# Ranking the experts behind the first gather, and letting the first pair of experts take turns from its first chunk

## The chip, the cores and the metric

The kernel runs on one core of a Trainium2 chip. The metric is the time of one execution on the device, in microseconds (us), median of several runs. Matrix products run on TensorE (PE in the profile, its weight loads PEld), elementwise work on VectorE (DVE) and ScalarE (ACT), a little on GpSimd (POOL). SyncE (SP) issues the loads of the weights; ScalarE also issues some stores.

## The reference

Two decoder layers over 256 tokens of width 1024. Layer 0 is gated linear attention and a dense SwiGLU, layer 1 is softmax attention with a forget gate ("fox") and a mixture of 8 experts, two of which serve each token. Each sub-layer has a norm ahead of it with a shift and a scale, and a gate on its residual. The change lies in the experts:

```python
def swiglu(h, w_gate, w_up, w_down):
    return (jax.nn.silu(h @ w_gate) * (h @ w_up)) @ w_down

def moe_swiglu(h, w_router, b_router, w_gate, w_up, w_down):
    logits = (h @ w_router).astype(jnp.float32) + b_router.astype(jnp.float32)
    top_vals, top_idx = lax.top_k(logits, TOP_K)
    top_w = jax.nn.softmax(top_vals, axis=-1)
    combine = jnp.sum(jax.nn.one_hot(top_idx, N_EXPERTS, dtype=jnp.float32)
                      * top_w[..., None], axis=-2)
    y = jnp.zeros_like(h)
    for e in range(N_EXPERTS):
        y = y + combine[..., e:e + 1].astype(h.dtype) * swiglu(h, w_gate[e], w_up[e], w_down[e])
    return y
```

Every expert has a gate and an up matrix of 1024 x 3584 and a down matrix of 3584 x 1024, all float32: 42 MB an expert, 336 MB for all 8 (1 MB = 2^20 bytes).

## The kernel before

The kernel does not compute all tokens with every expert. For each expert it gathers the tokens that chose it into up to 128 slots (large) or up to 64 slots (small), runs the SwiGLU on these, and scatters the result back with the weights of the router. The experts are put into 8 places: place 0 is always expert 0, taken as a large one; the other places are filled by rank, so that places 0, 2, 4, 6 are large and 1, 3, 5, 7 small. Which expert stands in a place is known on the chip only, in the tile `order`; the loads of the weights of place 1 and of all later ones take the expert's number from there, by a load into a register of SP at line 1264 (in `Slot.__init__`).

`route` (line 974) makes the router's logits (`lg`), the mask of the two largest (`msk`), each token's slot within its expert (`pos`), the rows of the tokens as a high and a low part (`hh`, `hl`), and, in `weights` (lines 1035 to 1078), the softmax weights (`comb`), the count of tokens per expert (`cnt`, by two small matmuls at line 1048), the rank of each expert, `order`, the slots and weights in the order of the places (`pos_s`, `comb_s`), and the room of each place (`room`, `cmi`), from which the kernel decides at its end whether a slow path is needed.

`experts` (line 1093) does the rest. `onehot` (line 1111) and `gather` (line 1123) put the tokens of a place into the operand `g` (large) or `gs` (small). The gather of place 0 uses `pos` and needs no rank; that of place 1 uses `pos_s`.

Weights come in units of 1 MB, one load each (`unit`, line 203), into a ring of 10 buffers (7 in one pool, 3 in another that opens with the experts), taken in the order in which the units stand in the program. The feed-forward width is cut into 4 chunks, three of 1024 columns and one of 512. For a large place `gu(c)` (line 1272) is the gate and up products of a chunk: 4 gate units and 4 up units (2 and 2 for the last chunk); `down(c)` (line 1300) is 4 units (2 for the last). Each unit is split into a high part on ScalarE (`whi`, line 224) and a low part, mostly on VectorE (`wlo`, line 226); the split ends the use of its buffer. There are 3 such pairs of parts. A unit is then 12 matmuls of 512 columns (lines 241 to 243). For a small place TensorE reads the unit as it is, in 8 matmuls (line 1249), and these end the use of the buffer. `finish` (line 1229) transposes a chunk's result for the down product; it is put off by `pend` and `flush` to the first unit of the next gate product. The first four splits have an order of their own (`hows`, line 1254), so that they fit around the router and the first gather.

The order of instructions on each engine is set by a planner, which goes through them by priority (the order of the program, with functions marked `urgent` moved up by 400) and by the times that it expects. `after(x)` lets an instruction follow `x` on `x`'s own engine.

In the first pair, places 0 and 1, the order of the program is: gate and up of chunk 0 and of chunk 1 for place 0, then `weights`, the down product of chunk 0, the gather of place 1, and only then place 1's chunk 0; from there the places take turns, place 0 one chunk ahead. The later pairs take turns from their first chunk on.

Of the kernel before, what the change touches and what calls it, by code (L numbers as in the profile page):

```python
# [8 lines left out]
F32 = mybir.dt.float32  # L9
# [15 lines left out]
NCH = 4  # L25
E = 8
# [24 lines left out]
def trunk(ctx, tc, x, c, ada_w, ada_b, norm_gain, gla_w_in, gla_w_gate_up, gla_b_gate, gla_o_norm, gla_w_out,  # L51
          fox_w_in, fox_b_f, fox_q_norm, fox_k_norm, fox_w_out, ffn_w_gate, ffn_w_up, ffn_w_down,
          moe_w_router, moe_b_router, moe_w_gate, moe_w_up, moe_w_down, out):
    nc = tc.nc
# [13 lines left out]
    def urgent(f):  # L68

        def g(*a, **k):  # L70
            with tc.high_priority(URGENT):
                return f(*a, **k)
        return g

    @contextmanager
    def after(*instructions):

        with ExitStack() as es:
            for i in instructions:
                es.enter_context(tc.issue_after(i.ins))  # L80
            yield
# [37 lines left out]
    bias = adap.tile([P, 96], F32, name="bias")  # L119
# [854 lines left out]
    def route(norm, wr):  # L974
        mp = wk
        first = {}
        msk, comb, pos = (cst.tile([P, NB, E], F32, name=n) for n in ("msk", "comb", "rpos"))
        cmi = cst.tile([P, 1], I32, name="cmi")
        order = cst.tile([P, E], I32, name="order")
        comb_s, pos_s = (cst.tile([P, NB, E], F32, name=n) for n in ("comb_s", "pos_s"))  # L980
        room = cst.tile([P, E], F32, name="room")
        hh, hl = (t.rearrange("p k t -> p (k t)")[:, 0:NB * D].rearrange("p (b d) -> p b d", b=NB)
                  for t in pair("Y", "m"))
        lg = mp.tile([P, NB, E], F32, tag="rlg", name="rlg", bufs=1)
# [47 lines left out]
                    nc.vector.scalar_tensor_tensor(hl[:, b, c], ps[2 * b + q], r[:, b:b + 1],  # L1032
                                                   hh[:, b, c].bitcast(F32), op0=ALU.mult, op1=ALU.subtract)

        def weights():
            mx = mp.tile([P, NB], F32, tag="rmx", name="rmx", bufs=1)
            sm = mp.tile([P, NB], F32, tag="rsm", name="rsm", bufs=1)
            nc.vector.tensor_reduce(mx, lg, axis=AX.X, op=ALU.max, negate=True)
            for b in range(NB):
                nc.scalar.activation(comb[:, b, :], lg[:, b, :], AF.Exp, bias=mx[:, b:b + 1])  # L1040
            nc.vector.tensor_mul(comb, comb, msk)
            nc.vector.tensor_reduce(sm, comb, axis=AX.X, op=ALU.add)
            nc.vector.reciprocal(sm, sm)
            for b in range(NB):
                nc.vector.tensor_scalar(comb[:, b, :], comb[:, b, :], sm[:, b:b + 1], None, op0=ALU.mult)
            cps_ = wk_ps("cnt")
            for b in range(NB):
                nc.tensor.matmul(cps_[:, 0:E], ones, msk[:, b, :], start=(b == 0), stop=(b == NB - 1))
            cnt, rank, u = (mp.tile([P, E], F32, tag="rk" + n, name="rk" + n, bufs=1) for n in "cru")
            m, t = (mp.tile([P, E, E], F32, tag="rk" + n, name="rk" + n, bufs=1) for n in "mt")  # L1050
            nc.vector.tensor_copy(cnt, cps_[:, 0:E])
            nc.vector.tensor_copy(u, cnt)
            nc.vector.memset(u[:, 0:1], -1.0)
            li, lj = u.unsqueeze(2).to_broadcast([P, E, E]), u.unsqueeze(1).to_broadcast([P, E, E])
            nc.vector.tensor_tensor(m, lj, li, op=ALU.is_equal)
            nc.vector.tensor_mul(m, m, tie)
            nc.vector.tensor_tensor(t, lj, li, op=ALU.is_lt)
            nc.vector.tensor_add(m, m, t)
            nc.vector.tensor_reduce(rank, m, axis=AX.X, op=ALU.add)

            nc.vector.tensor_tensor(m, rank.unsqueeze(1).to_broadcast([P, E, E]),
                                    srank.rearrange("p a b -> p (a b)").unsqueeze(2).to_broadcast([P, E, E]),
                                    op=ALU.is_equal)
            nc.vector.tensor_mul(t, m, iota_r[:, 0:E].unsqueeze(1).to_broadcast([P, E, E]))
            nc.vector.tensor_reduce(u, t, axis=AX.X, op=ALU.add)
            nc.vector.tensor_scalar(order, u, -1.0, None, op0=ALU.add)
            for to, of in ((pos_s, pos), (comb_s, comb)):
                for b in range(NB):
                    nc.vector.tensor_mul(t, m, of[:, b, :].unsqueeze(1).to_broadcast([P, E, E]))
                    nc.vector.tensor_reduce(to[:, b, :], t, axis=AX.X, op=ALU.add)  # L1070
# [20 lines left out]
        return rest, hh, hl, pos, comb, cmi, weights, first, order, pos_s, comb_s, room  # L1091

    def experts(norm, wr):
        rest, hh, hl, pos, comb, cmi, weights, first, order, pos_s, comb_s, room = route(norm, wr)
# [60 lines left out]
        oh0 = onehot(0, 0, pos)  # L1155
        xres = rest()
        urgent(gather)(0, 0, oh0)

        acts = {}

# [213 lines left out]
        for e in range(0, E, 2):  # L1374
            x = Large(e)
            x.gu(0)
            tail()
            if e == 0:
                x.gu(1)
                with after(acts["i"]):  # L1380
                    weights()
                x.down(0)
                gather(1, 1)
            y = Small(e + 1)
            y.gu(0)
            for c in range(NCH - 1):
                if e:
                    x.down(c)
                    x.gu(c + 1)
                    y.down(c)  # L1390
                    y.gu(c + 1)
                else:
                    x.down(c + 1, flush if c == NCH - 2 else lambda: None)
                    if c < NCH - 2:
                        x.gu(c + 2)
                    y.down(c)
                    y.gu(c + 1)
            if e + 2 < E:
                gather(e + 2, e + 3)
            if e:  # L1400
                x.down(NCH - 1, flush if e + 2 == E else lambda: None)

            def tail(y=y):
                y.down(NCH - 1, flush)
# [134 lines left out]
    with wk.phase("fox"):  # L1539
        n3 = Norm("moe", "X", lambda: mod[1, 4], lambda: mod[1, 3])  # L1540
        wr = side_by_side(small["wr_raw"], E, "wr")
# [3 lines left out]
        with tc.tile_pool(name="rawq", bufs=NRING - 7) as more["p"], wk.phase("experts"):  # L1545
            xres, hh, hl, pos, comb, cmi, room = experts(n3, wr)
# [31 lines left out]
```

## Time and profile before

| | us |
|---|---|
| median of 3 runs | 1489.23 (1488.38 to 1492.67) |
| the profiled execution | 1489.47 |
| its span, first to last instruction | 1487.8 |

| engine | busy us | share of the span |
|---|---|---|
| PE | 1417.3 | 95% |
| PEld | 1066.4 | 72% |
| DVE | 962.8 | 65% |
| ACT | 698.8 | 47% |
| POOL | 80.3 | 5% |

The span is cut into 40 slices of 37.2 us. The experts begin with the 17th slice, at about 595 us. Busy shares are means over stages with different limits; matmuls overlap one another, so a busy PE is not yet PE at its peak. Below, a row of a timeline is start, duration, engine, line, operation, out<-in, shape, and the number of instructions that were merged into it.

### The profile page before, as it was taken

Reading aid. Unit: us, or ns where it says so; the run is one execution under the profiler, and the core shown is the slowest. Engines: PE = TensorE matmul, PEld = TensorE weight load, DVE = VectorE, ACT = ScalarE, POOL = GpSimd, SP = SyncE. Lnnn points to the kernel's source line nnn. Section 1 sums busy time; section 2 is a strip of 40 time slices with the busy share of each in tenths; the row PEclk is TensorE's granted clock in tenths of the full one; section 3 lists DMA queues with packets and bytes.
Section 4 is the critical chain, followed back from the end, with each engine's and each line's share of the span. In section 5 each row is a group of like instructions: output and inputs, shape, how many; then the busy total and the mean of one; then the engine's idle time right before and its main releaser. Section 6 shows DMA issues by size and latency. Waiting matters only on the chain.

```text
span 1487.8 us, 21637 instructions
## 1 busy us (share of the span) xinstructions
PE 1417.3 (95%) x8443; PEld 1066.4 (72%) x8443; DVE 962.8 (65%) x1292; ACT 698.8 (47%) x984; POOL 80.3 (5%) x87
## 2 busy tenths in 40 slices
PE   6999999999999997999999999989999999999996
PEld 2899999999999997867445574656574556475453
DVE  7887897778977777757334672645574556574353
ACT  3654644334566455756223462544363445354241
POOL 2000200000132123000000000000000000000000
PEclk9999999999999997999999999999999999999998
DMA  9996579898954325569999999999999999999994
GB/s 318 362 350 234 173 281 324 314 324 283 286 164 149 131 97 198 198 238 409 407 405 402 408 409 409 409 403 402 409 408 409 409 402 403 409 409 408 409 396 184
DMA packets 183000, 488.86 MB, mean 329 GB/s; under 512 B 10815, under 2 KB 51913, under 8 KB 182890
## 3 DMA queue, kind: packets, MB, share of 16 engines
q1 hardware_dynamic: 182602, 486.87, 87.1%
q8 instruction: 68, 1.11, 0.3%
q10 hardware_dynamic: 288, 0.52, 0.1%
q14 instruction: 42, 0.34, 0.1%
HBM read 486.32 MB, written 1.05 MB: 328 GB/s over the span
## 4 chain that ended last, share of the span: by engine, by line
PE 78%; DMA 11%; DVE 7%; ACT 1%; issue 1%; SPq 1%; DVEq 0%; ACTq 0%
DMA raw<-in_moe_w_down_dram 7%; PE mo L243 6%; PE mo L241 6%; PE mo L242 6%; PE md L1249 6%; PE mo L1249 6%; DMA raw<-in_moe_w_up_dram 4%; PE md L243 3%; PE gu L247 3%; DVE wlo L226 3%; PE gu L249 3%; PE gu L248 3%; PE md L242 3%; PE md L241 3%; PE dn L247 2%; PE dn L248 2%
## 5 line engine op out<-in xcount | busy, mean ns | idle before, releaser
L226 DVE TENSOR_TENSOR wlo<-raw,whi 128x1024 fp32r<-128x1024 f32 (+2 forms) x481 | 570.2, 1232 | 84.1 <-ACT whi L224 82.4
L224 ACT CAST whi<-raw 128x1024 fp32r<-128x1024 f32 (+2 forms) x491 | 488.1, 1051 | 289.3 <-DMA raw<-in_moe_w_down_dram 101.0
L1249 PE MATMUL mo<-raw,gs 128*64 128x512 f32 (+1 forms) x1024 | 206.6, 544 | 19.6 <-DMA raw<-in_moe_w_up_dram 16.3
L241 PE MATMUL mo<-whi,g 128*128 128x512 f32 x448 | 176.1, 393 | 1.7 <-ACT msg L1293 1.3
L242 PE MATMUL mo<-whi,g 128*128 128x512 f32 x448 | 175.3, 392 | 0.0
L1249 PEld LDWEIGHTS mo<-raw,gs 128*64 128x64 f32 x1024 | 68.4, 136 | 145.3 <-issue 83.5
L243 PE MATMUL mo<-wlo,g 128*128 128x512 f32 x448 | 151.5, 398 | 1.2 <-DVE wlo L226 0.6
L1345 DVE TENSOR_TENSOR msg<-msg,mo 128x512 f32<-128x512 f32 (+1 forms) x16 | 9.9, 619 | 196.6 <-PE mo L1249 189.9
L243 PEld LDWEIGHTS mo<-wlo,g 128*128 128x128 f32 x448 | 83.2, 189 | 33.6 <-issue 11.4
L1249 PE MATMUL md<-raw,gs 128*64 128x512 f32 x448 | 106.5, 603 | 0.0
L241 PEld LDWEIGHTS mo<-whi,g 128*128 128x128 f32 x448 | 84.7, 189 | 20.1 <-ACT msg L1293 1.9
L242 PEld LDWEIGHTS mo<-whi,g 128*128 128x128 f32 x448 | 84.7, 189 | 17.8
L322 DVE SCALAR_TENSOR_TENSOR adacc<-raw,csil,adacc 128x1024 f32<-128x1024 f32 x70 | 90.1, 1286 | 8.3 <-DMA raw<-in_ada_w_dram 7.9
L249 PE MATMUL gu<-h_ffn_h,wlo 128*128 128x256 f32 x320 | 90.5, 284 | 0.0
L248 PE MATMUL gu<-h_ffn_l,whi 128*128 128x256 f32 x320 | 90.1, 282 | 0.0
L247 PE MATMUL gu<-h_ffn_h,whi 128*128 128x256 f32 x320 | 89.9, 283 | 0.0
L241 PE MATMUL md<-whi,act_h 128*128 128x512 f32 x192 | 76.8, 400 | 1.0 <-ACT whi L224 1.0
L242 PE MATMUL md<-whi,act_l 128*128 128x512 f32 x192 | 75.9, 395 | 0.0
L1343 ACT ACTIVATE msg<-mo 128x512 f32<-128x512 f32 (+1 forms) x16 | 8.7, 544 | 142.7 <-PE mo L1249 142.7
L1249 PEld LDWEIGHTS md<-raw,gs 128*64 128x64 f32 x448 | 27.9, 136 | 51.3 <-issue 51.1
L243 PE MATMUL md<-wlo,act_h 128*128 128x512 f32 x192 | 61.0, 398 | 1.6 <-DVE wlo L226 1.3
L248 PE MATMUL dn<-act_l,whi 128*128 128x256 f32 x224 | 62.2, 283 | 0.0
(489 smaller groups left out, 2648.0 us busy)
## 6 DMA issues: line engine op xcount, KB each, us to landing
raw<-in_moe_w_gate_dram SPq DMA_DIRECT2D x112, 1024.0 KB, 18.2
raw<-in_moe_w_up_dram SPq DMA_DIRECT2D x112, 1024.0 KB, 18.1
raw<-in_moe_w_down_dram SPq DMA_DIRECT2D x112, 1024.0 KB, 18.2
raw<-in_ada_w_dram SPq DMA_DIRECT2D x48, 1024.0 KB, 7.2
raw<-in_fox_w_in_dram SPq DMA_DIRECT2D x16, 1024.0 KB, 6.4
raw<-in_ffn_w_gate_dram SPq DMA_DIRECT2D x14, 1024.0 KB, 5.9
raw<-in_ffn_w_up_dram SPq DMA_DIRECT2D x14, 1024.0 KB, 6.7
raw<-in_ffn_w_down_dram SPq DMA_DIRECT2D x14, 1024.0 KB, 5.3
```

The lines of the kernel that those rows point to most:

```text
L224: nc.scalar.copy(hi[:, s], raw[:, s])
L226: (nc.gpsimd if i in pool else nc.vector).tensor_tensor(lo[:, s], raw[:, s], hi[:, s].bitcast(F32), op=ALU.subtract)
L241: nc.tensor.matmul(ps, ah, wh, start=first, stop=False)
L242: nc.tensor.matmul(ps, al, wh, start=False, stop=False)
L243: return nc.tensor.matmul(ps, ah, wl, start=False, stop=last)
L247: i = nc.tensor.matmul(ps, wh, ah, start=first, stop=False)
L248: nc.tensor.matmul(ps, wh, al, start=False, stop=False)
L249: nc.tensor.matmul(ps, wl, ah, start=False, stop=last)
L322: nc.vector.scalar_tensor_tensor(a, raw[:, kk, :], csil[:, k:k + 1], a, op0=ALU.mult, op1=ALU.add)
L1249: nc.tensor.matmul(ps[64 * i:64 * (i + 1), 0:n], a, w[:, i * n:(i + 1) * n], start=first, stop=last)
L1343: nc.scalar.activation(sg, ps[:, 0:hw], AF.Silu)
L1345: nc.vector.tensor_mul(sg, sg, ps[:, 0:hw])
```

## The change

`weights` is cut in two. The part that leads from the mask to `order` and `pos_s` becomes `ranks`, marked `urgent`, and is called right behind the gather of place 0. The softmax weights, `comb_s` and the room stay in `weights`, which is now called in the first turn of the first pair, without `after`. The helper `in_slots` is the old loop over `pos` and `comb`. In the first pair the special order is gone: behind chunk 0 of place 0 come the gather of place 1 and its chunk 0, and from there both pairs of the code are one.

```diff
-        def weights():
...
+        cnt, rank, u = (mp.tile([P, E], F32, tag="rk" + n, name="rk" + n, bufs=1) for n in "cru")
+        m, t = (mp.tile([P, E, E], F32, tag="rk" + n, name="rk" + n, bufs=1) for n in "mt")
+
+        def in_slots(to, of):
+            for b in range(NB):
+                nc.vector.tensor_mul(t, m, of[:, b, :].unsqueeze(1).to_broadcast([P, E, E]))
+                nc.vector.tensor_reduce(to[:, b, :], t, axis=AX.X, op=ALU.add)
+
+        @urgent
+        def ranks():
             cps_ = wk_ps("cnt")
             for b in range(NB):
                 nc.tensor.matmul(cps_[:, 0:E], ones, msk[:, b, :], start=(b == 0), stop=(b == NB - 1))
...
             nc.vector.tensor_scalar(order, u, -1.0, None, op0=ALU.add)
-            for to, of in ((pos_s, pos), (comb_s, comb)):
...
+            in_slots(pos_s, pos)
+        def weights():
...
+            in_slots(comb_s, comb)
...
         urgent(gather)(0, 0, oh0)
+        ranks()
...
             x.gu(0)
             tail()
             if e == 0:
-                x.gu(1)
-                with after(acts["i"]):
-                    weights()
-                x.down(0)
                 gather(1, 1)
             y = Small(e + 1)
             y.gu(0)
             for c in range(NCH - 1):
-                if e:
-                    x.down(c)
-                    x.gu(c + 1)
-                    y.down(c)
-                    y.gu(c + 1)
-                else:
-                    x.down(c + 1, flush if c == NCH - 2 else lambda: None)
-                    if c < NCH - 2:
-                        x.gu(c + 2)
-                    y.down(c)
-                    y.gu(c + 1)
+                x.down(c)
+                x.gu(c + 1)
+                if (e, c) == (0, 0):
+                    weights()
+                y.down(c)
+                y.gu(c + 1)
             if e + 2 < E:
                 gather(e + 2, e + 3)
-            if e:
-                x.down(NCH - 1, flush if e + 2 == E else lambda: None)
+            x.down(NCH - 1, flush if e + 2 == E else lambda: None)
```

## Rows read from the trace of the kernel before

**Rows 1.** The page's 40 slices: busy share of the DMA engines, GB/s.
```profile
DMA  9996579898954325569999999999999999999994
GB/s 318 362 350 234 173 281 324 314 324 283 286 164 149 131 97 198 198 238 409 407 405 402 408 409 409 409 403 402 409 408 409 409 402 403 409 409 408 409 396 184
```

**Rows 2.** Table of stretches: length, busy by engine (PE first), clock, DMA share, GB/s.
```profile
620.00:630.00 10.00, 10.00 (x52) 8.35 (x51) 9.04 (x10) 7.35 (x9) 0.00 (x0) 1.00 0.56 222
630.00:640.00 10.00, 8.75 (x39) 6.81 (x38) 7.97 (x20) 8.94 (x13) 0.00 (x0) 1.00 0.01 2
640.00:650.00 10.00, 10.00 (x45) 8.13 (x44) 10.00 (x17) 7.80 (x9) 0.00 (x0) 1.00 0.28 84
...
650.00:1456.00 806.00, 770.92 (x3553) 463.95 (x3553) 430.14 (x466) 350.02 (x432) 0.00 (x0) 1.00 1.03 406
```

**Rows 3.** The chain of waits near 716 us: start, duration, what.
```profile
716.51 18.33 DMA raw<-in_moe_w_down_dram
```

**Rows 4.** Timeline of SP's queue, the loads of the expert weights.
```profile
502.80 24.07 SPq L203 DMA_DIRECT2D raw<-in_moe_w_gate_dram  x4
...
564.04 0.37 SPq L203 DMA_DIRECT2D raw<-in_moe_w_gate_dram  x1
577.30 0.37 SPq L203 DMA_DIRECT2D raw<-in_moe_w_up_dram  x1
...
590.07 19.85 SPq L203 DMA_DIRECT2D raw<-in_moe_w_up_dram  x4
613.34 7.64 SPq L203 DMA_DIRECT2D raw<-in_moe_w_down_dram  x4
646.12 2.98 SPq L203 DMA_DIRECT2D raw<-in_moe_w_gate_dram  x4
```

**Rows 5.** Waits of SP's queue: total us, times, longest.
```profile
SPq L1264 <- DVE rkt L1069: 24.5, 1, 24.5
```

**Rows 6.** Timeline of VectorE; in brackets idle time before, and what ended it.
```profile
589.92 0.73 DVE L1149 TENSOR_SCALAR gs<-ga,mod,mod 128x128 f32<-128x128 f32 x2
...
601.21 2.50 DVE L226 TENSOR_TENSOR wlo<-raw,whi 128x512 fp32r<-128x512 f32 x4 [4.78 <-ACT whi L224]
...
620.51 1.28 DVE L1295 TENSOR_TENSOR msg<-msg,mo 128x512 f32<-128x512 f32 x2
...
630.86 0.16 DVE L1051 COPY rkc<-cnt 128x8 f32<-128x8 f32 x1
...
637.33 0.22 DVE L1058 TENSOR_TENSOR rkm<-rkm,rkt 128x64 f32<-128x64 f32 x1
637.59 0.22 DVE L1059 TENSOR_REDUCE rkr<-rkm 128x8 f32<-128x64 f32 x1
...
645.18 0.17 DVE L1066 TENSOR_SCALAR order<-rku 128x8 int32<-128x8 f32 x1
```

**Rows 7.** Timeline of TensorE: small matmuls, a large chunk, the start of place 1.
```profile
586.24 0.57 PE L1021 MATMUL pos<-msk,u_str 128*128 128x8 f32 x2
...
594.49 0.65 PE L1174 MATMUL oht<-ident,oh 128*128 128x128 f32 x2
...
602.43 0.39 PE L243 MATMUL mo<-wlo,g 128*128 128x512 f32 x1
...
603.11 0.39 PE L243 MATMUL mo<-wlo,g 128*128 128x512 f32 x1
...
655.62 0.31 PE L1131 MATMUL ga<-oh,m_h 128*128 128x64 f32 x2
...
657.42 1.08 PE L1249 MATMUL mo<-raw,gs 128*64 128x512 f32 x4
...
659.43 1.94 PE L1249 MATMUL mo<-raw,gs 128*64 128x512 f32 x8
...
662.31 1.94 PE L1249 MATMUL mo<-raw,gs 128*64 128x512 f32 x8
```

**Rows 8.** Timeline of ScalarE: a table load.
```profile
608.10 1.28 ACT L1293 ACT_TABLE_LOAD   x1
```

More of the change, by code (lines that the diff above doesn't have):

```diff
@@ L1033, in tokens @@
                                                    hh[:, b, c].bitcast(F32), op0=ALU.mult, op1=ALU.subtract)
-        def weights():
-            mx = mp.tile([P, NB], F32, tag="rmx", name="rmx", bufs=1)
-            sm = mp.tile([P, NB], F32, tag="rsm", name="rsm", bufs=1)
-            nc.vector.tensor_reduce(mx, lg, axis=AX.X, op=ALU.max, negate=True)
+        cnt, rank, u = (mp.tile([P, E], F32, tag="rk" + n, name="rk" + n, bufs=1) for n in "cru")
+        m, t = (mp.tile([P, E, E], F32, tag="rk" + n, name="rk" + n, bufs=1) for n in "mt")
+        def in_slots(to, of):
             for b in range(NB):
[L1040 to L1045, printed above, removed]
+                nc.vector.tensor_mul(t, m, of[:, b, :].unsqueeze(1).to_broadcast([P, E, E]))
+                nc.vector.tensor_reduce(to[:, b, :], t, axis=AX.X, op=ALU.add)
+        @urgent
+        def ranks():
             cps_ = wk_ps("cnt")
@@ L1048, in weights @@
                 nc.tensor.matmul(cps_[:, 0:E], ones, msk[:, b, :], start=(b == 0), stop=(b == NB - 1))
-            cnt, rank, u = (mp.tile([P, E], F32, tag="rk" + n, name="rk" + n, bufs=1) for n in "cru")
-            m, t = (mp.tile([P, E, E], F32, tag="rk" + n, name="rk" + n, bufs=1) for n in "mt")
             nc.vector.tensor_copy(cnt, cps_[:, 0:E])
@@ L1066, in weights @@
             nc.vector.tensor_scalar(order, u, -1.0, None, op0=ALU.add)
-            for to, of in ((pos_s, pos), (comb_s, comb)):
-                for b in range(NB):
-                    nc.vector.tensor_mul(t, m, of[:, b, :].unsqueeze(1).to_broadcast([P, E, E]))
-                    nc.vector.tensor_reduce(to[:, b, :], t, axis=AX.X, op=ALU.add)
+            in_slots(pos_s, pos)
+        def weights():
+            mx = mp.tile([P, NB], F32, tag="rmx", name="rmx", bufs=1)
+            sm = mp.tile([P, NB], F32, tag="rsm", name="rsm", bufs=1)
+            nc.vector.tensor_reduce(mx, lg, axis=AX.X, op=ALU.max, negate=True)
+            for b in range(NB):
+                nc.scalar.activation(comb[:, b, :], lg[:, b, :], AF.Exp, bias=mx[:, b:b + 1])
+            nc.vector.tensor_mul(comb, comb, msk)
+            nc.vector.tensor_reduce(sm, comb, axis=AX.X, op=ALU.add)
+            nc.vector.reciprocal(sm, sm)
+            for b in range(NB):
+                nc.vector.tensor_scalar(comb[:, b, :], comb[:, b, :], sm[:, b:b + 1], None, op0=ALU.mult)
+            in_slots(comb_s, comb)
             nc.vector.tensor_scalar(u, rank, 0.5, -64.0, op0=ALU.is_gt, op1=ALU.mult)
@@ L1089, in rest @@
             return residual_out(xps, first["hi"])
-        return rest, hh, hl, pos, comb, cmi, weights, first, order, pos_s, comb_s, room
+        return rest, hh, hl, pos, comb, cmi, weights, ranks, first, order, pos_s, comb_s, room
     def experts(norm, wr):
-        rest, hh, hl, pos, comb, cmi, weights, first, order, pos_s, comb_s, room = route(norm, wr)
+        rest, hh, hl, pos, comb, cmi, weights, ranks, first, order, pos_s, comb_s, room = route(norm, wr)
         a, s = norm.a(), norm.s()
```

## Prediction

> **What bounds the kernel now.** I read the views in this order: the page's slices, a table of stretches, the DMA queue's own timeline and waits, then VectorE and TensorE around the one hole that these show.
>
> The slices show a plateau: from the 19th slice to the last but one the DMA engines move about 405 GB/s and are full [rows 1]. The table of stretches says the same of 650 to 1456 us: 406 GB/s, DMA share 1.03 [rows 2]. TensorE is busy 770.92 of these 806 us, so both are nearly full; which of them ends last is seen where they part: at 716.51 us the chain of waits rests 18.33 us on a transfer of down weights [rows 3], and TensorE's missing 35 us are such waits. So I take the transfers as the bound of the expert stage. A unit is one weight tile of 128 x 2048 floats, 1.049 MB, and 406 GB/s make it 2.58 us; 8 experts have 336 units. Every one must pass, so the end is set by when the plateau starts and how many units are still to come.
>
> Ahead of the plateau there is a hole: 222 GB/s at 620 to 630 us, 2 GB/s at 630 to 640, 84 at 640 to 650 [rows 2]. The queue's timeline shows why. Loads are issued in the order of the program: 4 gate and 4 up units of the first large expert (called units 0 to 7; the last up unit at 577.30), 4 + 4 of its second chunk (units 8 to 15, from 564.04 to about 610), 4 down units (16 to 19, from 613.34), and then nothing until 646.12 [rows 4]. In between SP waits 24.5 us at line 1264, the load of the small expert's number from `order` into a register [rows 5] (the row names line 1069 as releaser; the instruction that writes `order` is the one just ahead of it). `order` is written at 645.18 to 645.35 [rows 6], 0.77 us before the first load that uses it. So in the kernel before 20 units are issued ahead of the wait and 316 behind it.
>
> **The change part by part.** The new emission is: ranks behind the first gather, large chunk 0, gather of the small expert, small chunk 0, and so on. Three things follow.
>
> 1. The wait for `order` moves ahead of the ninth unit. Units 0 to 7 are issued as before; units 8, 9, 10, 11, 12, which before went out between 564.04 and 590.07 [rows 4], now stand behind the register load. That is the price: 12 units fewer are issued ahead of the wait, 12 x 2.58 = 31.0 us of transfer that must now be done after it. The gain is that the wait ends earlier. If t is the first issue behind it, the saving is 646.12 - t - 31.0, and the two are even at t = 615.1.
>
> 2. When is t? `ranks` needs two small matmuls (the count) and then 12 VectorE instructions down to `order`. The operands are ready (the mask is older than the positions), but the count's PSUM tile comes behind the four of the gather, so its matmuls go to TensorE behind the gather, which ends with the transposes of the one-hot at 594.49 [rows 7]. Two matmuls of that size took 0.57 a pair of passes at the granted clock of that stretch [rows 7], so 1.1 us, and 0.65 for the transposes if these go first: the counts are there at 595.7 to 596.2. VectorE has 4.78 us without work up to 601.21, since the split of the fourth unit waits for TensorE [rows 6]; that hides the chain. Its step from one dependent instruction to the next is 0.26 us (637.33 to 637.59 [rows 6]), 12 of them 3.1 us: `order` at about 599.2. With the 0.77 us from `order` to the first issue, t = 600.0. Saving: 46.1 - 31.0 = 15.1 us. Were that cover gone, each us of VectorE's split work ahead of the chain would cost one us. The four instructions of `in_slots(pos_s)` and the one-hot of the small expert follow in the same gap, five times about 0.3 us, and nobody waits for them before 620. Bounds of t: not before 595.5, since the count's PSUM tile is free when the first gather tile has been read at about 590.7 [rows 6] (590.7 + 1.1 + 3.1 + 0.77, rounded down); not after 610.8, if the chain is woven between the splits as now, where it took 14.3 us from 630.86 to 645.18 [rows 6]. I take 600.0 because the idle row covers the whole chain.
>
> 3. Does the plateau hold once it has begun? Five units have a free buffer at t; units 13 to 17 take buffers that the large expert's splits free, as before, from 603.7 to about 617 [rows 4]. Ten units last 25.8 us, to about 627 with the latency. Unit 18 now needs the buffer of unit 8, a small-expert unit, which TensorE frees. The large chunk is done by 620.51, when VectorE multiplies its gate and up halves [rows 6]; before, the gather of the small expert began at 655.62 and its first unit (the 4 matmuls ahead, half of the 8 at 659.43) was through at 660.4 [rows 7], 4.8 us later. So unit 18 can go at 625.3, just in time. The next buffers come 2.5 to 2.9 us apart while gather and matmuls alternate (659.43 to 662.31 [rows 7]), against 2.58 us of transfer: I charge 0.7 us. Behind that the small units are consumed in 1.94 us each (8 matmuls [rows 7]) and the large ones in 2.72 us (12 matmuls; three of them from 602.43 to 603.11 take 0.68 [rows 7]), and the turns mean 2.3, so buffers come faster than transfers. This also caps a gain from an earlier t: with unit 18 at 625.3 the saving is 646.12 - 625.3 - 2 x 2.58 = 15.6 us, and 18.5 if TensorE has done the gather earlier and unit 18 goes at 620.5 + 1.94.
>
> Nothing for the rest. `weights` keeps its instructions, and its result is first read by the first scatter, behind the last down chunk of the pair. Without the ordering edge its exponential may go anywhere on ScalarE; an early table load (1.28 us at line 1293 [rows 8]) could push TensorE's start by one to three us, which shifts step 3 and not t; the lower end of that is nothing, and I take nothing. The first mo tile may share a bank with the count and wait for its copy: 0 to 1 us, same place. The end of the first pair gets the shape of the later pairs, whose stretches run at the same 406 GB/s; zero, with the plateau as cover. The tail is untouched.
>
> Sum: 15.1 - 0.7 = 14.4 us. The profiled execution took 1489.47 us, its span is 1487.8; 1489.47 - 14.4 = 1475.1. The median of the runs is 0.24 lower than that execution, so I forecast 1474.8.
>
> A page speaks for a smaller gain. The plateau row says 406 GB/s [rows 2]. The Trainium skill, page "DMA: Bandwidth & Descriptors", section Specifications, gives about 358 GB/s as what HBM leaves one core; by that a unit would be 2.93 us (an estimate from that page), the 12 units 35.1 us, and the time about 1479. This trace disagrees for over 800 us, and the measurement decides.
>
> **The rivals.**
>
> Late ranks (slower than before). The list of each engine is written by a planner, and it does reorder: unit 8 went out ahead of unit 7 [rows 4]. If the count's matmuls or the chain stand behind the first large chunk, as they stood behind the second one before (count read at 630.86 [rows 6]), `order` comes after 620.51. Then t = 620.5 + 1.1 + 3.1 + 0.77 = 625.5, the saving is 20.6 - 31.0 = -10.4, and the time 1499.6. It decides from t = 615.1 on. Against it: `ranks` has the raised priority of the gather, and its operands are ready.
>
> Woven ranks. The chain starts at 595.7 but waits between splits: t up to 610.8, saving down to 4.3, time 1478 to 1485. Against it stands the idle row of VectorE.
>
> TensorE is the bound. It is busy 96% from 650 on; if its order of work and not the transfers set the end, filling the hole only moves where units wait, and what remains is its idle time around the hole, 1.25 us at 630 to 640 [rows 2]: time 1488. Against it: its 35 us of idle time are waits for transfers, and the plateau does not dip when its work gets lighter.
>
> The small expert frees buffers sooner (more gain): the cap of 18.5 us, time 1470.7.
>
> **How the numbers follow.** A measurement of this kernel tells about 0.3%, 4.5 us, from no change: 1484.8 to 1493.7. Forecast, saving 11 to 17 us: 0.68. More, to 20 us: 0.07. Woven ranks, 4.5 to 11 us: 0.09. Around no change (TensorE as the bound, or t near 613): 0.08. Slower by late ranks: 0.08. So faster 0.84, same 0.08, slower 0.08. The range from 1470.0 (the cap) to 1484.0 (woven ranks) leaves out about 0.18.
>
> **What would show it.** SP's wait at the register load now lies ahead of the ninth unit and ends near 600; the stretches from 602 to 650 move about 400 GB/s with at most a small notch near 625; the last weights land 14 to 15 us earlier and the tail is as long as before. Wrong are: `order` written after 605 (step 2), a hole at 620 to 640 (step 3), or a plateau below 400 GB/s with TensorE without waits (the bound).

## Result and profile after

| | before | after |
|---|---|---|
| median of 5 runs, us | 1489.56 (1488.38 to 1492.67) | 1479.04 (1474.76 to 1479.23) |
| the profiled execution, us | 1489.47 | 1478.52 |
| its span, us | 1487.8 | 1476.8 |

The ratio is 0.9914, with a 95% interval of 0.989 to 0.9938: the change makes the kernel faster by 10.5 us. Forecast were 1474.8 us and a range of 1470.0 to 1484.0. The sign and the range held; the median lies 4.2 us above the forecast, and a good part of what follows is about where these 4 us are.

SP's queue in the kernel after; each row is start, duration, engine, line, operation, tiles, and the number of loads merged into it:

```profile
506.82 7.51 SPq L203 DMA_DIRECT2D raw<-in_moe_w_gate_dram  x2
...
603.32 2.27 SPq L203 DMA_DIRECT2D raw<-in_moe_w_gate_dram  x4
605.83 8.46 SPq L203 DMA_DIRECT2D raw<-in_moe_w_up_dram  x4
617.71 3.95 SPq L203 DMA_DIRECT2D raw<-in_moe_w_down_dram  x2
...
628.81 0.37 SPq L203 DMA_DIRECT2D raw<-in_moe_w_down_dram  x1
...
1435.97 6.90 SPq L203 DMA_DIRECT2D raw<-in_moe_w_down_dram  x4
```

The row of the kernel before that answers to the last one, its final four down loads:

```profile
1446.68 6.83 SPq L203 DMA_DIRECT2D raw<-in_moe_w_down_dram  x4
```

SP's wait at the register load, line 1271 in the kernel after (total us, times, longest; the row names an instruction just behind the one that writes `order`):

```profile
SPq L1271 <- DVE rku L1079: 21.4, 1, 21.4
```

Read against [rows 4]: the wait for the expert's number now stands ahead of the ninth unit, and the first load behind it goes at 603.32, where it went at 646.12. Unit 18, the first that needs a small expert's buffer, goes at 628.81. The whole picture is shifted, though: the first gate load of the experts is at 506.82, against 502.80 in [rows 4]. So times are best read from that load on. From it to the first of the last four down loads the kernel before takes 1446.68 - 502.80 = 943.88 us, the kernel after 1435.97 - 506.82 = 929.15. The difference is 14.73 us; the forecast for it was 14.4.

The table of stretches of the kernel after (length, busy by engine with PE first, granted clock, DMA share, GB/s):

```profile
590.00:600.00 10.00, 9.14 (x43) 8.81 (x43) 7.33 (x22) 5.48 (x12) 0.52 (x1) 0.50 0.01 2
600.00:605.00 5.00, 5.00 (x13) 3.92 (x14) 4.63 (x28) 0.05 (x1) 0.00 (x0) 0.53 0.15 20
605.00:610.00 5.00, 5.00 (x24) 4.14 (x23) 3.69 (x6) 4.13 (x6) 0.00 (x0) 1.00 0.97 387
610.00:620.00 10.00, 10.00 (x50) 8.43 (x49) 6.99 (x7) 8.87 (x11) 0.00 (x0) 1.00 1.02 412
620.00:630.00 10.00, 10.00 (x55) 7.01 (x55) 2.54 (x4) 1.40 (x4) 0.00 (x0) 1.00 1.03 410
630.00:640.00 10.00, 10.00 (x52) 3.96 (x48) 7.68 (x7) 6.95 (x9) 0.00 (x0) 1.00 1.00 381
640.00:650.00 10.00, 10.00 (x43) 5.73 (x42) 3.21 (x4) 3.29 (x5) 0.00 (x0) 1.00 1.02 411
650.00:1456.00 806.00, 780.31 (x3601) 481.47 (x3600) 448.52 (x476) 366.64 (x448) 0.00 (x0) 1.00 1.02 405
```

The hole of [rows 2] at 620 to 650 (222, 2, 84 GB/s) is full: 410, 381, 411. In its place stands the one at 590 to 605, which the price of the moved wait put there. The 381 is the notch at unit 18. The plateau moves 405 GB/s, against 406 in [rows 2].

VectorE, where the chain from the count to `order` lies:

```profile
599.63 0.17 DVE L1048 COPY rkc<-cnt 128x8 f32<-128x8 f32 x1 [0.32 <-PE cnt L1047]
...
602.44 0.17 DVE L1063 TENSOR_SCALAR order<-rku 128x8 int32<-128x8 f32 x1
...
605.60 2.50 DVE L226 TENSOR_TENSOR wlo<-raw,whi 128x512 fp32r<-128x512 f32 x4 [0.73 <-ACT whi L224]
```

The chain takes 2.8 us from the start of the copy to the start of the write of `order`, and `order` is there 3.0 us before the next split (605.60 - 602.61), which still waits for ScalarE: the idle time of [rows 6] covers it whole.

TensorE's shares in it:

```profile
598.73 0.86 PE L1047 MATMUL cnt<-msk,ones 128*128 128x8 f32 x4
...
599.95 0.76 PE L241 MATMUL mo<-whi,g 128*128 128x512 f32 x1
...
626.83 5.37 PE L1256 MATMUL mo<-raw,gs 128*64 128x512 f32 x24
```

The count went between the two transposes of the one-hot; the first large product starts at 599.95, which is 595.93 on the clock of the kernel before (506.82 - 502.80 = 4.02 taken off) and 0.34 later than there (595.59). The first small product begins at 626.83.

### The profile page after: what moved, and what is told of

The parts are those of the page before. It is cut to its first block, busy times and chain, and to the rows that moved or that the text cites. A ratio compares the mean times of both kernels' runs of the same rounds, so it can differ in the third digit from the quotient of the medians.

```text
span 1476.8 us, 21633 instructions
## 1 busy us (share of the span) xinstructions
PE 1419.3 (96%) x8443; PEld 1073.4 (73%) x8443; DVE 961.7 (65%) x1292; ACT 695.1 (47%) x982; POOL 80.5 (5%) x87
## 4 chain that ended last, share of the span: by engine, by line
PE 81%; DMA 9%; DVE 7%; issue 1%; SPq 1%; ACT 0%; DVEq 0%; ACTq 0%
PE mo L1256 8%; PE mo L243 6%; PE mo L241 6%; PE mo L242 6%; PE md L1256 6%; DMA raw<-in_moe_w_up_dram 4%; PE gu L247 3%; DVE wlo L226 3%; PE gu L249 3%; PE gu L248 3%; PE md L243 3%; DMA raw<-in_moe_w_down_dram 3%; PE md L242 3%; PE md L241 3%; PE dn L247 2%; PE dn L248 2%
## 5 line engine op out<-in xcount | busy, mean ns | idle before, releaser
L1175 ACT CAST act_h<-actT 128x512 fp32r<-128x512 f32 x24 | 13.3, 589 | 116.2 <-PE actT L1240 116.2
```

The lines of the kernel that those rows point to most:

```text
L1175: acts["i"] = nc.scalar.copy(ah, v)
```

## Experiments

All times below are medians with the range of the runs, and each ratio, with its 95% interval, is against runs of the kernel before made beside it on the same chip (its medians: 1490.25 for e1 to e4, 1490.44 for e5 to e8, 1491.54 for e9 to e11). For each profiled execution the table has the stages of SP's queue: the first gate load of the experts, the first load behind the expert's number, unit 18, the first of the last four down loads, and the last less the first, the length of the stream.

| kernel | first gate | behind the number | unit 18 | last four | stream |
|---|---|---|---|---|---|
| before | 502.80 | 646.12 | | 1446.68 | 943.88 |
| after | 506.82 | 603.32 | 628.81 | 1435.97 | 929.15 |
| e1 ranks alone | 506.93 | 628.48 | | 1440.97 | 934.04 |
| e2 late ranks | 506.78 | 628.35 | | 1459.44 | 952.66 |
| e3 no wait | 506.85 | | 629.37 | 1438.40 | 931.55 |
| e4 order later | 503.93 | 612.24 | | 1443.10 | 939.17 |
| e5 order earlier | 506.92 | 597.96 | 629.36 | 1436.44 | 929.52 |
| e6 second gather early | 502.62 | 599.11 | 626.73 | 1432.48 | 929.86 |
| e7 both | 507.11 | 598.14 | 630.53 | 1440.37 | 933.26 |
| e8 the change again | 506.99 | 603.49 | 629.37 | 1436.66 | 929.67 |
| e9 change, wide columns | 502.75 | 599.25 | 625.00 | 1432.55 | 929.80 |
| e10 before, wide columns | 501.25 | 644.88 | | 1446.03 | 944.78 |
| e11 the change beside e9 | 502.30 | 598.80 | 624.42 | 1431.91 | 929.61 |

**e1, one half alone.** The ranks are early, the order of the first pair is the old one:

```diff
             if e == 0:
+                x.gu(1)
+                with after(acts["i"]):
+                    weights()
+                x.down(0)
                 gather(1, 1)
...
+                else:
+                    x.down(c + 1, flush if c == NCH - 2 else lambda: None)
```

> One part of the change alone: the ranks right behind the first gather, but the first pair in the old order (two chunks of the large place, then its first down product, then the small place). All times against 1489.4 us of before. Theory (transfers are the bound, and the ring of 10 buffers lets them run ahead only as far as buffers come free): 20 units go out ahead of the register load as before, the wait at the load is gone, but the large units free a buffer only every 2.72 us and the unit numbered 30 waits for the first small unit, at about 657 to 660 us; saving (646.1 - 660) + 10 x 2.58 = 12 to 15 us, so 1474 to 1478, less up to 4 us if the stretch ahead of the experts runs late in this kernel as it does in the changed one. Rival A (the early rank is worth nothing without the turns, because the ring is full of large units): at most 4 us faster, 1485 or more. Rival B (the wait is lost time as a whole): all of its 24.5 us come back, 1465. Rival C (TensorE is the bound): about 1488.

Measured: 1483.45 us (1478.39 to 1485.56), 0.9936 (0.9911 to 0.9961). The stream is 9.84 us shorter than before, not 14.73. `order` is there as early as in the kernel after (602.6), but the queue asks for it only at 628.48:

```profile
617.73 7.64 SPq L203 DMA_DIRECT2D raw<-in_moe_w_down_dram  x4
628.48 10.53 SPq L203 DMA_DIRECT2D raw<-in_moe_w_gate_dram  x4
```

and what it waited for until then is the splits of large units (its waits from 590 to 660: total, times, longest):

```profile
SPq L203 <- DVE wlo L226: 52.9, 16, 13.6
```

So the early ranks alone bring two thirds of the gain. The turns bring the rest, but only behind early ranks: with late ranks the same turns lose 8.8 us (e2). That they gain because small units between the large ones free buffers in another way fits the waits above, but no run separates it. The gain is a little under what my theory gave, far above rival A and far below B.

**e2, the rival on the other side.** The turns as in the change, but `ranks` without its raised priority, and the count's matmuls held behind the last matmul of the first large chunk:

```diff
-        @urgent
         def ranks():
...
-        ranks()
...
+                with after(first['end']):
+                    ranks()
```

> The other part alone: the turns from the first chunk on, but the count's matmuls held behind the last matmul of the large place's first chunk, so that the number of the small place comes late. Theory: the first load behind the register load goes out at t = 625.5 (629.5 if the start is 4 us late as in the changed kernel), the saving is 646.1 - t - 31.0, so -10.4: 1500 us (1504 with the late start), and the transfers stand still from about 581 to 626 us. Rival (TensorE is the bound, transfers have slack): TensorE loses only the wait for the gather and the first small unit, about 6 to 8 us against the changed kernel: 1485 to 1487.

Measured: 1499.68 us (1495.14 to 1502.20), 1.0052 (1.0031 to 1.0073). The first load behind the number is at 628.35, 121.57 behind the first gate load; the forecast for this rival was 625.5 - 502.80 = 122.7. The stream is 8.8 us longer than before, against 10.4 worked out. The turns without early ranks lose: the price of the moved wait is real, and the sign hangs on when `order` comes.

**e3, the wait taken away.** The first loads of place 1 take a fixed expert, and the number is fetched behind them:

```diff
-            y = Small(e + 1)
+            if e == 0:
+                y = Small(0)
+                y.e = 1
...
             y.gu(0)
+            if e == 0:
+                y.number()
```

> The changed kernel, but the gate and up loads of the first chunk of the small place take a fixed expert (number 0) and so wait for no rank; the register load comes behind them. That part of the output is another expert's. Theory (step 3, the cap): units 8 to 12 go out at 564 to 590 us as in the kernel before, but unit 18 still waits for the first small unit at about 625 (629 with the late start), so only 1 to 4 us are gained on the changed kernel: 1475 to 1478 against 1479. Rival (the 12 units held back cost their whole 31.0 us, or what the transfers stand still between 581 and 603): 20 us or more faster, 1459 or less.

Measured: 1477.70 us (1474.71 to 1480.30), 0.99 (0.9861 to 0.9939). Units 8 to 12 go out as in the kernel before, and still the stream is 2.4 us longer than after the change. The stretches show where the head start goes (columns as above):

```profile
590.00:600.00 10.00, 9.14 (x44) 8.81 (x43) 7.32 (x23) 5.45 (x12) 0.55 (x1) 0.50 0.70 243
600.00:605.00 5.00, 5.00 (x12) 3.93 (x13) 4.66 (x28) 0.03 (x1) 0.00 (x0) 0.50 0.00 0
605.00:610.00 5.00, 5.00 (x22) 4.05 (x21) 3.14 (x5) 3.91 (x6) 0.00 (x0) 0.92 0.12 19
610.00:625.00 15.00, 15.00 (x75) 12.61 (x74) 8.80 (x8) 9.57 (x13) 0.00 (x0) 1.00 0.93 313
625.00:630.00 5.00, 5.00 (x29) 3.01 (x29) 4.35 (x5) 4.48 (x8) 0.00 (x0) 1.00 0.39 121
```

The five units that pass early leave a hole of their own at 600 to 610, then the loads run at the pace of the large splits (313 GB/s), and at 625 they run dry (121 GB/s): unit 18 goes at 629.37, 122.5 behind the first gate load, as in the kernel after (122.0). So the cap of step 3 is there: by unit 18 all that was won ahead of it is given back. It does not make the stream longer than after the change, though. The 2.4 us lie later, where the loads of e3 thin out more than those of the kernel after; first e3, then the kernel after:

```profile
690.00:695.00 5.00, 5.00 (x26) 1.67 (x24) 0.63 (x2) 0.00 (x0) 0.00 (x0) 1.00 0.52 170
```

```profile
685.00:690.00 5.00, 5.00 (x24) 1.44 (x20) 0.96 (x2) 0.00 (x0) 0.00 (x0) 1.00 0.98 348
690.00:695.00 5.00, 5.00 (x28) 2.20 (x28) 1.29 (x2) 1.08 (x2) 0.00 (x0) 1.00 0.94 357
```

The kernel before has no such dip there (410 and 408 GB/s). What holds the loads back at that place was not followed.

**e4, `order` later.** Fourteen multiplications by one on GpSimd stand between the ranks and `order`:

```diff
-            nc.vector.tensor_scalar(order, u, -1.0, None, op0=ALU.add)
...
+            for i in range(14):
+                nc.gpsimd.tensor_tensor(d, d, ones, op=ALU.mult)
+            nc.vector.tensor_scalar(order, d[:, 0:E], -1.0, None, op0=ALU.add)
```

> The changed kernel with the number of the small place made later: between the rank and its conversion stand 14 small multiplications by one on GpSimd, which has no other work there; some 6 to 8 us. Nothing else waits for it. Theory: the time follows t one for one (less the 0 to 2 us in which the ring would have run dry anyway): 6 to 8 us slower than the changed kernel, 1484 to 1487. Rival (slack in the ring, or TensorE as the bound): no slower than the changed kernel, 1479 to 1480.

Measured: 1485.92 us (1482.53 to 1489.65), 0.9964 (0.9946 to 0.9982). The first load behind the number is 108.31 behind the first gate load, against 96.50 after the change: 11.8 later. The stream is 10.0 longer. So late is paid nearly one for one; the 1.8 us between may be the thin stretches, which a late stream does not meet (it moves 409 GB/s at 630 to 640). The delay itself was mis-sized: the 14 multiplications took 10.7 us where 6 to 8 were expected. That the median still lies within the expected 1484 to 1487 is luck, since this kernel lost less ahead of the experts (first gate load at 503.93; 4 of its 10 runs under a mean clock of 0.987, where the kernel after had 4 of 5).

**e5, `order` earlier.** The count and its chain ahead of the first gather:

```diff
+        ranks()
         urgent(gather)(0, 0, oh0)
-        ranks()
```

> The changed kernel with the count of the ranks and the order of the experts ahead of the first gather instead of right behind it. The order should be written some 3 us earlier relative to the first gate load, the gather some 0.9 us later. Theory (the cap: from the order on the stream stops at unit 18, whose buffer comes free with the first small unit, so an order that is early leaves only the thin stretch of 1.25 us to fill or to lose): 1477.5 to 1479.5 at an equal start, so within 1.5 us of the changed kernel run beside it. Rival A (one for one, as with the late order): 3 us faster, near 1476. Rival B (the later gather sets the first small unit later): 0.9 to 2 us slower, near 1480.5. The stretch ahead of the experts can run up to 4 us late by the granted clock; compared at the same first gate load.

Measured: 1478.86 us (1473.30 to 1479.95), 0.991 (0.9891 to 0.9929). The first load behind the number is 5.5 us earlier (91.04 behind the first gate load; about 3 were expected), unit 18 is not (122.4), and the stream is the same within 0.4 us. The transfers run dry ahead of unit 18 instead:

```profile
625.00:630.00 5.00, 5.00 (x29) 3.02 (x29) 3.56 (x4) 3.95 (x7) 0.00 (x0) 1.00 0.26 103
```

With e4: later costs, earlier gives nothing. The change sits at the knee.

**e6, the second gather early.** An attempt to move the cap: place 1's gather gets the raised priority.

```diff
-                gather(1, 1)
+                urgent(gather)(1, 1)
```

> The changed kernel with the second place's gather moved ahead of other ready work on TensorE, the order where the change has it. Theory: the buffer of unit 18, which waits for the first unit of a small expert, comes free some 2.9 us earlier, and the thin stretch that costs the changed kernel 1.25 us is filled: 0.5 to 1.5 us faster than the changed kernel run beside it, near 1478. Rival A (the thin stretch is not set by that buffer): the same as the changed kernel within 0.3 us. Rival B (the gather taken ahead pushes the first large units back, and their buffers with them): 1 to 3 us slower.

Measured: 1478.29 us (1474.94 to 1480.74), 0.9922 (0.9904 to 0.9939). My theory falls. The small place's first full run of matmuls:

```profile
624.77 6.23 PE L1256 MATMUL mo<-raw,gs 128*64 128x512 f32 x28
```

That is 122.15 us behind the first gate load; in the kernel after it is 626.83 - 506.82 = 120.01. (Two matmuls of the first small unit went at 621.72, but its other six, and with them its buffer, belong to this run.) TensorE is busy 5.00 of 5.00 us in every stretch from 600 to 625 of both kernels, so what is put ahead there pushes the large chunk back: its last matmuls start 121.83 behind the first gate load (624.45), in the kernel after 118.43 (625.25). The small chunk follows it, and unit 18 goes 2.1 us later, not 2.9 earlier. The stream is 0.2 to 0.7 us longer than in the two executions after, e8 included.

**e7, both.** The edits of e5 and e6 together, meant as a version that beats both kernels.

> Both: the order ahead of the first gather, and the second place's gather early. Theory: the early order alone runs into the buffer of unit 18, and the early buffer alone has only 1.25 us to give; together the order is 3 us earlier and the buffer that it would wait for is 2.9 us earlier (less 0.9 for the later first gather), so 2.5 to 4 us faster than the changed kernel run beside it, near 1475 at an equal start. Rival A (something else limits the stretch behind the order, such as the large units' own buffers): no more than 1.5 us faster, 1477.5 to 1479. Rival B (what is put ahead on TensorE delays the first units): slower by 1 us or more.

Measured: 1477.49 us (1476.09 to 1482.46), 0.9907 (0.9887 to 0.9927). The median is the lowest of e5 to e8, and yet the stream is 4.1 us longer than after the change. The loads behind the number:

```profile
598.14 2.46 SPq L203 DMA_DIRECT2D raw<-in_moe_w_gate_dram  x4
600.93 16.19 SPq L203 DMA_DIRECT2D raw<-in_moe_w_up_dram  x4
```

The four up loads take 16.19 us where the kernel after takes 8.46: with the second gather among its matmuls the large chunk frees its buffers later. Rival B holds. The median misleads because three of its four runs had a high mean granted clock; at 0.988 it has 1477.07 and 1477.92, the change itself 1474.30 to 1475.29 (4 runs).

**e8, the change again.**

> The changed kernel itself again, beside the kernel before on the same chip. Theory: what its profiled execution lost against the forecast (4.02 us, all of it ahead of the first gate load) belongs to the execution and not to the change, so the times spread over some 1474 to 1480 with the granted clock, the profiled one's first gate load lies anywhere from 503 to 507, and 1456.0 plus or minus 1 us minus the first 503 holds from that load on: 975 to 977 us to the end of the span. Rival (the change itself makes the stretch ahead late): first gate load at 506 or later again, and no run under 1477.

Measured: 1478.55 us (1473.49 to 1484.03), 0.9913 (0.9889 to 0.9937). The 975 to 977 us in the expectation is a slip of arithmetic: from the first gate load to the end of the span the execution after takes 1476.8 - 506.82 = 970.0, this one 1477.5 - 506.99 = 970.5. The first gate load was late again, but runs of 1473.49 and 1474.40 stand beside runs of 1478 and 1479.6, and e6, which has the whole change in it, has its first gate load at 502.62 and its time at 1474.94. So the late start comes and goes with the execution.

**Where the late start is made.** Far ahead of the experts the kernel before has these rows (columns as above; the sixth figure behind the comma is the granted clock):

```profile
138.00:140.00 2.00, 2.00 (x19) 2.00 (x18) 1.36 (x4) 0.00 (x0) 0.00 (x0) 1.00 0.00 0
140.00:142.00 2.00, 2.00 (x19) 2.00 (x19) 0.04 (x1) 1.91 (x1) 0.00 (x0) 1.00 0.00 0
```

and the kernel after these:

```profile
136.00:138.00 2.00, 2.00 (x14) 1.95 (x13) 0.50 (x3) 0.84 (x4) 0.00 (x0) 0.77 1.01 386
138.00:140.00 2.00, 2.00 (x11) 2.00 (x11) 0.24 (x2) 0.04 (x1) 0.70 (x1) 0.50 0.13 49
140.00:142.00 2.00, 2.00 (x11) 2.00 (x11) 1.43 (x4) 0.16 (x1) 0.00 (x0) 0.50 0.00 0
142.00:144.00 2.00, 2.00 (x12) 2.00 (x11) 0.00 (x0) 0.00 (x0) 0.00 (x0) 0.52 0.00 0
```

In the execution after, the clock goes from its upper level, 2.4 GHz, to the lower, 1.2 GHz, for some 7 us while TensorE counts as busy throughout, and 11 matmuls pass in 2 us instead of 19. Just ahead of it TensorE, in the kernel after, had run two groups of 16 matmuls that move one column each (its timeline):

```profile
134.34 1.84 PE L309 MATMUL adat<-ones,adacc 128*128 128x1 f32 x16
136.25 0.59 PE L613 MATMUL o<-gs,qb 128*128 128x256 f32 x2
136.68 3.04 PE L309 MATMUL adat<-ones,adacc 128*128 128x1 f32 x16
```

In the second group the 16 take 3.04 us instead of 1.84. The kernel before has the same groups (133.31 and 135.64, 1.84 each) and no fall. By the next such group, at 208.05 against 204.03, all 4.02 us are lost. What the change touches lies 450 us behind this point.

But this fall is not the whole loss. The first of the two groups already starts 1.03 us later than in the kernel before (134.34 against 133.31), and that comes from a fall ahead of it. First the kernel after:

```profile
38.00:40.00 2.00, 2.00 (x7) 1.24 (x8) 2.00 (x4) 0.86 (x2) 0.00 (x0) 0.52 1.10 348
40.00:42.00 2.00, 2.00 (x13) 2.00 (x12) 0.38 (x1) 1.41 (x3) 0.00 (x0) 0.62 1.11 367
```

then the kernel before, where the clock fell earlier and cost less:

```profile
30.00:32.00 2.00, 2.00 (x7) 0.48 (x6) 2.00 (x6) 0.00 (x0) 1.38 (x2) 0.55 1.14 316
32.00:34.00 2.00, 1.50 (x7) 0.57 (x6) 1.85 (x4) 0.36 (x1) 0.00 (x0) 0.59 1.18 300
```

The two falls go together. All seven profiled executions with the first gate load at 506.78 or later (the kernel after, e1, e2, e3, e5, e7, e8) have the fall at 38 to 42 and then the long one at 136 to 146. In the kernel before, e6 and e11 it fell at 30 to 38 and not at 136; in e9 and e10 at neither place; in e4 at 136 alone, for half as long. So what differs between the executions is there at 38 us, and the first of the one-column groups runs only at 104.

**e9, e10, e11, the late start.** The one-column matmuls move 64 columns, in the kernel after (e9) and in the kernel before (e10); e11 is the change itself beside them:

```diff
-                nc.tensor.matmul(ps[:, k:k + 1], a[:, k * P:(k + 1) * P], ones[:, 0:1], start=True, stop=True)
+                nc.tensor.matmul(ps[:, 64 * k:64 * k + 64], a[:, k * P:(k + 1) * P], ones[:, 0:64], start=True, stop=True)
```

> The changed kernel with one edit far ahead of the experts: the 144 matmuls that turn the sums of the modulation into columns move 64 columns of ones each instead of 1 (the result is read from the first of the 64). In the profiled execution of the changed kernel the granted clock fell to 0.50 between 138 and 142 us right behind two groups of 16 such one-column matmuls, with TensorE busy throughout, and the first gate load came at 506.82; where it did not fall, at 502.6 to 502.8. Theory (the one-column matmuls bring the clock down, and with it the late start): the clock stays at 1.00 from 120 to 150 us, the first gate load lies at 502.5 to 503.5, nearly all runs have a mean granted clock of 0.988 or more, and the median is 1474 to 1475.5. Rival A (the clock falls for another reason): first gate load at 506 or later in about half of the runs, median 1478 to 1479.5, as the changed kernel beside it. Rival B (64 columns cost TensorE time): every run 1 to 4 us longer.

> The kernel before with the same edit alone: 64 columns instead of 1 in the 144 matmuls of the modulation. Theory (the one-column matmuls bring the clock down in some executions): no run over 1491, median 1488 to 1489.5, against 1490 to 1490.5 of the kernel before beside it, and against the changed kernel with the same edit a difference of 14 to 15 us, the change without the late start in either. Rival A (another reason): runs between 1488 and 1495 as before. Rival B: every run 1 to 4 us longer.

> The changed kernel unchanged, as the one that the wide matmuls are compared with on the same chip. Expected of every theory: median 1478 to 1479.5 with single runs from 1473.5 to 1484, by the granted clock; if this chip grants the higher clock in most executions, the median moves towards 1475, and then the edit has little left to gain.

Measured:

| kernel | median, us | ratio | runs under a mean clock of 0.987 |
|---|---|---|---|
| e9 change, wide | 1475.47 (1474.37 to 1480.58) | 0.9899 (0.9877 to 0.9921) | 1 of 6 |
| e11 change | 1476.99 (1473.60 to 1479.69) | 0.9905 (0.9882 to 0.9928) | 3 of 6 |
| e10 before, wide | 1490.10 (1488.36 to 1492.22) | 0.9992 (0.9979 to 1.0005) | 0 of 12 |
| before | 1491.54 (1486.93 to 1496.02) | 1 | 5 of 17 |

The wide matmuls cost next to nothing (16 take 1.89 us, 16 narrow ones 1.84), so rival B falls. The profile of e9 is as its theory wants it: clock 1.00 from 120 to 150 us, first gate load at 502.75. Runs with the lower mean clock are 1 of 18 with the edit and 8 of 23 without. That would fit the narrow groups, but it does not show them to be the cause: the runs are few, the mean clock does not tell where in a run it fell, the profile of e11 has narrow groups (134.41 and 136.75) and a clock of 1.00 behind them, and the profiles of e9 and e10 have no fall at 30 to 42 us either, ahead of all that the edit touches. An execution that fell at 38 us with the wide matmuls in it was not caught. A bound that I gave for e10 did not hold: two of its runs are over 1491 (1491.77, 1492.22), and its median is over 1489.5. e9 has the lowest ratio of all runs that compute the whole result; its interval overlaps that of the change. With the wide matmuls on both sides, the change is worth 1490.10 - 1475.47 = 14.6 us.

## Why the prediction was right, and where it was not

**The price of the moved wait** was right: from the first load behind the number to the last four, 312 units took 800.56 us before, 2.566 each, so 12 units are 30.8 us (forecast 31.0).

**The time t** was right. On the clock of the kernel before the first load behind the number is at 603.32 - 4.02 = 599.30, against 600.0. The count's copy is at 595.61, the chain took 2.8 us (forecast 3.1), and from the end of the write of `order` to the load it is 603.32 - 602.61 = 0.71 (0.77). The two places that could have made it late, the count behind a chunk and the chain between the splits, are e2 and, by its price, e4.

**The ring** was right in its place and in its size. Unit 18 goes at 624.79 on that clock (forecast 625.3), and the notch behind it, 381 GB/s over 10 us where the stretch ahead has 410, costs 10 x (1 - 381 / 410) = 0.7 us, as charged. Over the whole stream the loss is 1435.97 - 603.32 - 324 x 2.566 = 1.3 us. The prediction has no line for the other dips; the deepest is the one at 685 to 695 shown under e3. The 1.25 us that e5 to e7 put down to the thin stretch at unit 18 are this loss of the whole stream. That earlier ranks give no more (e5) and that even no wait gives no more (e3) is this cap. What the text did not see is that taking the gather ahead does not lift the cap (e6), although it named that as the way to 18.5 us: TensorE was busy without a break there.

**The sum.** 46.82 us earlier, less 30.8, less 1.3: 14.7 (forecast 14.4; measured in the stream 14.73). The 1.3 is what is left over, so the sum closes of itself; what was tested are its first two terms. The repeats of the change, e8 and e11, have 14.2 and 14.3 against the same execution of before.

**Nothing for the rest** held. The tail, from the last four loads to the end of the span, is 40.83 us (41.12 before). The exponential ran at 587.37 with no table load of its own, and of the three table loads of the kernel before ([rows 8] and two more) one is left:

```profile
587.37 0.51 ACT L1070 ACTIVATE comb<-rlg,rmx 128x8 f32<-128x8 f32 x2
...
612.46 1.28 ACT L1300 ACT_TABLE_LOAD   x1
```

**TensorE as the bound** was wrong for the whole, since a later `order` cost its time (e2, e4), and is half right near the change. But the argument against it, that TensorE's missing 35 us are waits for transfers, was half wrong. Waits of PE from 650 to 1456 us (total, times, longest), the two largest before and then after:

```profile
PE mo L1249 <- DMA raw<-in_moe_w_up_dram: 15.5, 25, 0.8
PE actT L1355 <- DVE msg L1345: 10.5, 13, 0.9
```

```profile
PE actT L1362 <- DVE msg L1352: 10.5, 15, 0.9
PE mo L1256 <- DMA raw<-in_moe_w_up_dram: 8.4, 14, 0.8
```

With the gate loads (3.2 and 1.5 us) 18.7 of the 35 us were waits for transfers before, and 9.9 are after. The first long rest of the chain on a transfer has moved from [rows 3] (716.51) to

```profile
952.37 17.59 DMA raw<-in_moe_w_up_dram
```

and from 600 to 720 the chain of the kernel after is TensorE's work without a transfer. With the hole closed the two bounds lie close together; that speeding up one alone would give little is likely, but no run shows it.

**The step that failed** is one that stands in no line of its own: to take 14.4 us off the time of one profiled execution (1489.47 - 14.4) is to take it that all that lies ahead of the experts takes the time it took in that execution. It took 4.02 us more, 1.0 by the fall at 38 us and 3.0 behind 134 us. The account of the two profiled executions closes with it: -14.73 of stream, -0.29 of tail, +4.02 of start make -11.0, the difference of the spans. That the median lies in the forecast range all the same is owed to the width of the range: the terms of the sum came true, and a loss that stood in none of them took 4 of the 14 us. The loss lies outside what the change edits and goes with the clock: executions of before lie between 1486.36 and 1497.28, and at equal mean clock the two kernels differ as forecast. At 0.985 before has 1492.63 to 1495.76 (9 runs) and the change 1479.04, 1479.07, 1479.58 and 1479.62; at 0.988 before has 1489.59 and 1491.28, the change 1474.30 to 1475.29 (4 runs). What the change may do is to meet the falls more often: 11 of 17 of its runs lie under 0.987, of the kernel before 16 of 50. Whether it does, and how an edit of the experts could reach back to 38 and 136 us, stays open; the kernel before was profiled only once, without the late start.

**The page.** The measured plateau is 405 GB/s over 806 us of the kernel after, against 406 in [rows 2]. By the 358 GB/s of the Trainium skill, page "DMA: Bandwidth & Descriptors", section Specifications, the time was to be about 1479 by the estimate in the prediction, and the median is 1479.04; the rows show that this is an accident, since the rate is 405 and the 4 us lie ahead of the first load of the experts.

## What to carry to other kernels

Where one queue issues all loads in program order, a load that needs a value made on the chip stops all loads behind it (24.5 us before, 21.4 after): count the loads ahead of it, and price a move by units lost against microseconds won. An earlier value pays only up to the next limit, here the buffer that the ring needs next, and moving work ahead on an engine that was already full moved that limit the wrong way (e6, e7). Compare two executions from a common landmark as well as by their ends, and small differences at equal granted clock: a median over few runs can order two versions the wrong way round, as it did with e7.

## What the runs showed of the hardware

TensorE's granted clock fell to 0.50 for 3.4 us (e4) to 6.8 us (the kernel after) while the profile has it busy without a break, in some executions and not in others of the same kernel (the kernel after and e8 against e11). In all eight profiled executions with a fall between 136 and 146 us it fell in the second of two groups of 16 one-column matmuls or right behind it, and in seven of the eight it had also fallen at 38 to 42 us, ahead of any such group. With 64 columns fewer runs had a low mean clock (1 of 18 against 8 of 23); that the groups are the cause is not shown. In the eight, the first gate load of the experts came 1.1 (e4) to 4.3 us (e7) later than in the kernel before.

A unit of 1 MB went through in 2.57 us on average, over 312 units in a row before (800.56 us) and over 324 after (832.65 us), though the order of large and small ones differs between the two.
